# Weights of the RWKV loop brought in by GpSimd DMAs alone: high part cast on the way, low part accumulated from DRAM

## The chip, the cores and the metric

The kernel runs on one core of one Trainium2 chip. The metric is the device time of one execution in microseconds. The kernel before was timed three times: 1142.22, 1146.9 and 1147.43 us, median 1146.9 us.

## What is computed

One layer on 512 tokens of width 1024, all in float32. After an RMS norm one wide product `h @ w_in` gives receptance, keys, values, the two halves of a gated convolution, and two gates. The RWKV-7 time mix runs a recurrence over the tokens for 16 heads of 64 channels (`S = S*w + (S a) b + v k`, `y = S r`); the kernel does it in 8 chunks of 64 tokens. Beside it stands a causal convolution of 31 taps with layer norm and SiLU. Both branches are projected, gated and added; an output projection, a norm with residual, and a SwiGLU feed-forward with 2816 inner channels follow.

Float32 accuracy comes from splitting. A weight `w` is held as a high part `wh`, which is `w` rounded to float32r, and a low part `wl = w - wh`; an activation likewise as `rh + rl`. A product is `wh rh + wh rl + wl rh`: three matmuls of 128 x 128 weights against 128 x 512 activations.

## The kernel before

Channels are tiled by 128, so a product of depth 1024 is 8 such triples. `acc3` (lines 175 to 181) issues one triple: line 179 is `wh rh`, line 180 `wh rl`, line 181 `wl rh`. Weights come in halves: `wload` (lines 162 to 173) fetches 4 tiles side by side, 128 x 512 values or 256 KB, into the buffers `wh` and `wl`, of which there are four each (`WB = 4`). So a half serves 12 matmuls.

`wload` has two forms. Both have SP load the float32 values into a third buffer, `wf` (four of them). In the form used by the loop (`eng is G`), ScalarE (ACT) converts `wf` to `wh` (line 168), ACT writes `-wh` into `wl` (line 169), and a DMA issued by GpSimd (POOL) adds `wf` to it in place (line 170). In the other form ACT converts and VectorE (DVE) subtracts (`split`, lines 158 to 160). The loop's form is used for 106 halves, those whose nominal load position lies between `T0P = 0` and `T1P = 475`; in the trace they are loaded from 47 to 645 us. The start and everything after that use the other form.

The program between is written as a list of small functions with nominal positions (`plan`, `at`), sorted and emitted in that order. Per 128-channel tile there are 44 nominal units: decay, keys, receptance, values (three products of two halves each), masked products inside the chunks (lines 589 to 597), a triangular inverse on DVE (lines 634 and 638), and the chain over the chunks: matmul line 718, ACT copy line 721, matmul line 726, ACT copy line 738, matmul line 744, ACT copy line 751, then the next chunk. Convolution products and taps (line 844) are spread between. A half's load is placed `LEAD = 11` units ahead of its use, or after the last matmul of the half that had its buffers, whichever is later.

Those positions are priorities. Below them a framework orders each engine's instructions by when it expects their inputs, and places all semaphores; each engine then runs its own list strictly in order, and a DMA's wait is done by the engine that issues it.

Of the kernel before, what the change touches and what calls it, by code (L numbers as in the profile page):

```python
# [8 lines left out]
F32 = mybir.dt.float32  # L9
F32R = mybir.dt.float32r  # L10
I32 = mybir.dt.int32
AF = mybir.ActivationFunctionType
ALU = mybir.AluOpType
# [3 lines left out]
P = 128  # L17
# [12 lines left out]
WB = 4  # L30
NWO = 3
BUFS = (2, 2, 2, 2, 1, 1, 1)
# nominal positions that order the program
PERIOD = 44.0
NCL = 3
CPERIOD = 96.0
# [4 lines left out]
WBF = 4  # L41
# [57 lines left out]
def tile_hybrid_block(ctx, tc, xT, cst, prm, dwp, wl1, w2g, w_in, w_ro, w_co, w_o,  # L99
                      w_gt, w_up, w_dn, outT):  # L100
    nc = tc.nc
    V, G, S = nc.vector, nc.gpsimd, nc.scalar
# [9 lines left out]
    wp = ctx.enter_context(tc.tile_pool(name="wp", bufs=WB))  # L112
# [10 lines left out]
    def f(ap):  # L123
        return ap.bitcast(F32)

# [1 line left out]
    cs = cp.tile([P, NC], F32, name="cs")  # L127
    pr = cp.tile([P, NV * NT], F32, name="pr")
    dw = cp.tile([P, NT * KW], F32, name="dw")
# [8 lines left out]
    ones = cs[:, C_ONE:C_ONE + WS]  # L138
# [15 lines left out]

    E, O = slice(0, 64), slice(64, 128)

# [1 line left out]
    def split(src, hi, lo):  # L158
        S.activation(out=hi, in_=src, func=AF.Copy)  # L159
        V.tensor_sub(lo, src, f(hi))  # L160

    def wload(wap, nk, eng=None):
        wf = wp.tile([P, nk * P], F32, tag="wf", bufs=WBF, name="wf")
        wh = wp.tile([P, nk * P], F32R, tag="wh", name="wh")
        wl = wp.tile([P, nk * P], F32R, tag="wl", name="wl")
        nc.sync.dma_start(out=wf, in_=wap)
        if eng is G:
            S.activation(out=wh, in_=wf, func=AF.Copy)  # L168
            S.activation(out=wl, in_=f(wh), func=AF.Copy, scale=-1.0)  # L169
            G.dma_start(out=wl, in_=wf, accum_op=ALU.add)  # L170
        else:
            split(wf, wh, wl)
        return wh, wl

# [27 lines left out]
                     in_=r8.unsqueeze(2).to_broadcast([P, 8, HD]), func=AF.Copy)  # L202
        bcast(ps, lambda b: rx[:, b * P:(b + 1) * P])

    # 1 / sqrt(v) for v > 0: a first guess from the bits, then Newton's steps
    def rsqrt(v, n):
        y, t, w = (sp.tile([P, n], F32, tag=g_, bufs=2, name=g_) for g_ in ("ry", "rt", "rw"))
        V.tensor_scalar(out=y.bitcast(I32), in0=v.bitcast(I32), scalar1=-0.5, scalar2=RSQ,
# [21 lines left out]
        bcast(bc, lambda b: r[:, b:b + 1].to_broadcast([P, P]), blocks)  # L230
        return bc

# [1 line left out]
    ctx_h = ExitStack()  # L234
    hp = ctx_h.enter_context(tc.tile_pool(name="hp", bufs=1))
    HH = hp.tile([P, NT, T + 2], F32R, tag="s1", name="HH")
# [33 lines left out]
    for t_ in (HH, HL):  # L270
        G.memset(f(t_[:, :, 0:2]), 0.0)

    # mean square of x over the channels, per token
    acc = tmp("acc", "ys")

    def sumsq(acc, src, first, name):
# [4 lines left out]
            S.activation(out=sq, in_=src, func=AF.Square)  # L281
            V.tensor_add(acc, acc, sq)

    # the first products take x before its norm, and the norm after them
    ps3 = [p_.tile([P, T], F32, tag=g_, name="dn") for p_, g_ in ((pd, "dn"), (pd, "dn"), (py, "y"))]
    for k in range(NT):
        if k == WK:
# [20 lines left out]
                                   op0=ALU.mult, op1=ALU.mult)  # L308
            split(xs[:, k, :], hh(k), hl(k))

    # derived parameters
    V.tensor_scalar(out=drv[:, 0:3 * NT], in0=vecs("mu_r", 3), scalar1=-1.0, scalar2=1.0,
                    op0=ALU.mult, op1=ALU.add)
    V.tensor_scalar_mul(drv[:, 3 * NT:5 * NT], vecs("decay_w0", 2), 0.5)
# [1 line left out]
    V.tensor_scalar(out=drv[:, 6 * NT:7 * NT], in0=vecs("k_a"), scalar1=-0.5, scalar2=1.0,  # L316
                    op0=ALU.mult, op1=ALU.add)

# [1 line left out]
    ctx_w = ExitStack()  # L320
    Pbd = []
    kp = None
# [11 lines left out]
        nc.sync.dma_start(out=dw, in_=dwp)  # L334
        V.tensor_scalar_mul(dw, dw, 0.5)

    # low-rank inputs: (h + (h_prev - h) mu) W = h (W - mu W) + h_prev (mu W)
    low = {}

    def low_weights(g):  # L340
# [14 lines left out]
    def low_rank(g):  # L355
        t_ = low[g]
        lo_f = tmp("lo_f", "th") if g else ep_.tile([P, T], F32, name="lo_f")
        if g == 0:
            pa, pb_ = (pm.tile([P, T], F32, tag=g_, bufs=1, name="lora") for g_ in ("sb", "fi"))
            for k in range(NT):  # L360
                for q, ps in ((0, pa), (2, pb_)):
                    acc3(ps, t_[:, q, k, :], t_[:, q + 1, k, :], [k], lambda k: XH[:, k, :],
                         lambda k: XL[:, k, :], k == 0, k == NT - 1)
            sh = tmp("sh", "sq", 2)
            V.tensor_mul(lo_f, pa, bx)
            V.tensor_mul(sh, pb_, bx)
            V.tensor_add(lo_f[:, 1:T], lo_f[:, 1:T], sh[:, 0:T - 1])
            S.activation(out=lo_f[E], in_=lo_f[E], func=AF.Tanh)
            # the low parts beside the high ones, under the other half of the rows
            for X, R, Q in ((LH, E, O), (LL, O, E)):  # L370
                S.activation(out=X[R], in_=lo_f[R], func=AF.Copy)
                V.tensor_sub(X[Q], lo_f[R], f(X[R]))
        else:
            ps = pd.tile([P, T], F32, tag="dn", name="lora")
            for k in range(NT):
                for q, rh, rl in ((0, hh, hl), (2, hhs, hls)):
                    acc3(ps, t_[:, q, k, :], t_[:, q + 1, k, :], [k], rh, rl,
                         k + q == 0, k == NT - 1 and q == 2)
            S.activation(out=lo_f, in_=ps, func=AF.Tanh, scale=0.5)
            S.activation(out=lo_f, in_=lo_f, func=AF.Identity, scale=0.5, bias=0.5)  # L380
            split(lo_f, GH, GL)
# [44 lines left out]
    halves = []  # L426
# [21 lines left out]
                fns.append(lambda: then(d["ps"]))  # L448
            halves.append([ts, lambda eng, k0=k0: load(k0, eng), fns])

    # weights are loaded ahead of their use, as far as the buffers go
    def plan_halves():
        halves.sort(key=lambda e: e[0][0])
        for i, (ts, ld, fns) in enumerate(halves):
# [28 lines left out]
    def plan_decay(ct):  # L483
        s_ = st[ct]

        @at(ct, 0.0)
        def _():
            w2h, w2l = low_out(ct, 0, 2 * P, "w2")
            # decay: log w = -exp(-1/2) sigmoid(z)
            zw = pm.tile([P, T], F32, tag="sm", name="zw")  # L490
            low2(zw, w2h[:, 0:P], w2l[:, 0:P], E, LH)
            cum = ktmp("cum")
            S.activation(out=cum, in_=zw, func=AF.Tanh, scale=0.5, bias=der(D_W0H, ct))
            S.activation(out=cum, in_=cum, func=AF.Identity, scale=0.5, bias=0.5)
            V.tensor_tensor_scan(out=cum, data0=reset, data1=cum, initial=0.0,
                                 op0=ALU.mult, op1=ALU.add)
            ep = ktmp("ep", cols=NCH * (L + 1)).rearrange("p (c t) -> p c t", c=NCH)
            G.memset(ep[:, :, 0:1], 1.0)
            S.activation(out=ep[:, :, 1:L + 1], in_=ch3(cum), func=AF.Exp, scale=-C0)
            S.activation(out=cum, in_=cum, func=AF.Exp, scale=C0)  # L500
            dL = sp.tile([P, NCH], F32, tag="dL", bufs=3, name="dL")
            V.tensor_copy(out=dL, in_=ep[:, :, L])
            za = pm.tile([P, T], F32, tag="sm", name="za")
            low2(za, w2h[:, P:2 * P], w2l[:, P:2 * P], O, LL)
            tha = ktmp("tha")
            S.activation(out=tha, in_=za, func=AF.Tanh, scale=0.5, bias=der(D_A0H, ct))
            kf = ktmp("kf")
            S.activation(out=kf, in_=tha, func=AF.Identity, scale=der(D_KAH, ct),
                         bias=der(D_KAO, ct))
            s_.update(cum=cum, ep=ep, dL=dL, tha=tha, kf=kf)  # L510
# [65 lines left out]
    def plan_inner(ct):  # L576
        s_ = st[ct]

        # masked products inside the chunks
        def inner(hc, par):  # L580
            if hc == 0 and par == 0:
                s_["Mt"] = kp.tile([P, NCH, L], F32, tag="Mt", bufs=BUFS[4], name="Mt")
# [17 lines left out]
        for j, (hc, par) in enumerate(((0, 0), (0, 1), (1, 0), (1, 1))):  # L600
            at(ct, 2 * DL + 3.0 + 2.0 * j)(lambda hc=hc, par=par: inner(hc, par))

        # token-major keys
        @at(ct, 2 * DL + 2.0)
        def _():
            bkT = kp.tile([P, NCH, P], F32, tag="bkT", bufs=BUFS[2], name="bkT")
# [7 lines left out]
    def plan_solve(ct):  # L614
        s_ = st[ct]

        # inverse of (I - M) on the 32 x 32 diagonal blocks, one block column class per partition
        @at(ct, 2 * DL + 11.0)
        def _():
            Mt = s_["Mt"]  # L620
# [23 lines left out]
        def _():  # L644
# [3 lines left out]
                        in_=Ps.rearrange("p i q -> p q i"))  # L648
            P32T = kp.tile([P, NCH, B32], F32, tag="P32T", bufs=1, name="P32T")
            V.transpose(out=P32T.rearrange("p c t -> p (c t)"),  # L650
                        in_=P32.rearrange("p c t -> p (c t)"))
            # upper right block: P1 M12 P2
            Wt = kp.tile([P, NCH, B32], F32, tag="Ps", bufs=1, name="Wt")
            R1 = [slice(h * 64, h * 64 + 32) for h in range(2)]
            R2 = [slice(h * 64 + 32, h * 64 + 64) for h in range(2)]
# [20 lines left out]
    def plan_values(ct):  # L676
# [7 lines left out]
        else:  # L684
            plan_dense(ct * PERIOD + 2 * DL, DT, w_in[2 * NT + ct], values)

        # token-major values, centred over the head; bonus
        @at(ct, 3 * DL + 3.0)
        def _():
            tv = s_["bv"]  # L690
# [17 lines left out]
    def plan_chain(ct):  # L708
# [15 lines left out]
        def step1(c):  # L724
            UV, SV, pb, zt, zs = (s_[n] for n in ("UV", "SV", "pb", "zt", "zs"))
            u_ = [PE.matmul(zt[R, 1, :], lhsT=pb[R, c, :], rhs=zs[R], start=True, stop=True)  # L726
                  for R in (E, O)]
            # state before the chunk, under the update
            if 0 < c < NCH - 1:
                s_["old"] = [PE.matmul(zt[R, 2, :], lhsT=ident[R, par * 64:par * 64 + 64],  # L730
                                       rhs=SV[R, c, par, :], start=True,
                                       stop=False, skip_group_check=True)
                             for par, R in ((0, E), (1, O))]
                for a_ in s_["old"]:
                    for b_ in u_:
                        order(a_, b_)
            for par, R in ((0, E), (1, O)):
                S.activation(out=UV[R, c, par, :], in_=zt[R, 1, :], func=AF.Copy)  # L738
# [12 lines left out]
                    S.activation(out=SV[R, c + 1, par, :], in_=zt[R, 2, :], func=AF.Identity,  # L751
                                 scale=dL[R, c:c + 1])

        # output of the chunk
        def step3(c):
            AR, GR, UV, SV, yp = (s_[n] for n in ("AR", "GR", "UV", "SV", "yp"))
            seq = []
# [97 lines left out]
                   plan_chain, plan_finish, plan_conv):  # L855
            pl(ct)

# [1 line left out]
    QT = ("mu_k", "kkn", "tha", "cum", "kf", "ep", "mu_r", "mu_r")  # L859
    HALF = (slice(0, TH), slice(TH, T))  # L860

# [41 lines left out]
        plan_dense(TM + POST + 48 * DTZ * m + 24 * DTZ, DTZ, w_ro[m], lambda ps, m=m: out_r(m, ps),  # L903
                   lambda k: mid["YH"][:, k, :], lambda k: mid["YL"][:, k, :])

    # layer norm over the channels, silu
    TC = max(conv_at(NT - 1) + 2 * CPERIOD2 + 0.1, TM + 2.0)

    def chsum(k):
# [62 lines left out]
    mp = mid["mp"]  # L972
    mh, ml = (lambda k: MH[:, k, :]), (lambda k: ML[:, k, :])

# [1 line left out]
    mo = xp.tile([P, NT, T], F32, tag="x", name="mo")  # L976
    psn = [p_.tile([P, 2, NWO + 1, WS], F32, tag=g_, name="psn") for p_, g_ in ((pc, "ch"), (pm, "sm"))]
    acc = tmp("acc", "ys")
# [59 lines left out]
        residual(m, 0, bc)  # L1038
    bc = all_rstd(psn[1], RMS_EPS, 2)

# [1 line left out]
    psf = [p_.tile([P, T], F32, tag=g_, bufs=1, name="psf")  # L1042
           for p_, g_ in ((pm, "fi"), (pm, "sb"), (pc, "ch"), (py, "y"))]
    for k in range(NT):
# [30 lines left out]
    last = []  # L1075
# [108 lines left out]
```

## Time and profile before

| | |
|---|---|
| timed runs, median | 1146.9 us |
| the profiled execution, first to last instruction (span) | 1165.1 us |
| PE busy, share of the span | 1138.6 us, 98% |
| DVE busy | 721.4 us, 62% |
| ACT busy | 616.5 us, 53% |
| POOL busy | 96.2 us, 8% |
| mean granted TensorE clock | 0.950 of full |
| HBM read | 84.25 MB |

The profiled execution is 18.2 us longer than the median of the timed ones. The span falls into the start (to about 75 us), the loop with the chain (to about 500 us), the end of the loop where the last chain runs beside gate products (to 575 us), a dense stretch of gate and output products that still uses the loop's form of `wload` (to 645 us), and the rest, which the change does not touch. A busy PE is not a PE at its peak: matmuls overlap and their ends are modelled, so how far matmuls start apart says more than the busy time. The TensorE clock has two levels, 1.2 and 2.4 GHz; the granted clock of a stretch is the mean of the two as a share of the upper one.

### The profile page before, as it was taken

The numbers are of one execution on the slowest core, as the hardware profiler recorded it, in microseconds if no ns is written. First come the engines' busy times: TensorE is split into PE (matmuls) and PEld (weight loads), VectorE is DVE, ScalarE is ACT, GpSimd is POOL, SyncE is SP. The second block draws the span as 40 slices with busy tenths as digits, with TensorE's granted clock in tenths as the row PEclk, the third lists the DMA queues.
The fourth block names the chain that finished last, engine by engine and source line by source line (L and its number), as shares of the span: only waits on it lengthen the run. The fifth ranks groups of instructions, "written<-read, shape, count | busy, mean of one in ns | idle before, by whom it ended". The sixth has DMA issues, their size and how long they took to land.

```text
span 1165.1 us, 17942 instructions
## 1 busy us (share of the span) xinstructions
PE 1138.6 (98%) x6506; PEld 869.8 (75%) x6506; DVE 721.4 (62%) x1699; ACT 616.5 (53%) x1291; POOL 96.2 (8%) x140
## 2 busy tenths in 40 slices
PE   7999999999999999999999999999999999999996
PEld 5777675757676767677788788899888888888886
DVE  7968676747776748699698737546444444433324
ACT  6777776758756747564655724535333333333321
POOL 0111010101010101112222000000000000000000
PEclk9999988869988869899999999999999999999998
DMA  7145342524342423356798434500332322333322
GB/s 245 44 100 118 78 98 46 116 46 92 71 100 50 97 69 81 68 125 147 163 203 197 117 99 139 178 19 10 101 98 91 99 91 94 96 91 109 109 64 73
DMA packets 74202, 117.41 MB, mean 101 GB/s; under 512 B 15745, under 2 KB 21249, under 8 KB 74113
## 3 DMA queue, kind: packets, MB, share of 16 engines
q1 hardware_dynamic: 58848, 88.47, 25.2%
q0 software_dynamic: 15264, 27.79, 14.3%
q8 instruction: 51, 0.84, 0.3%
q14 instruction: 39, 0.31, 0.1%
HBM read 84.25 MB, written 2.10 MB: 74 GB/s over the span
## 4 chain that ended last, share of the span: by engine, by line
PE 91%; ACT 4%; DVE 3%; issue 1%; DMA 0%; SPq 0%; DVEq 0%; ACTq 0%
PE dn L179 22%; PE dn L181 22%; PE dn L180 22%; PE gps L589 3%; PE yp L759 2%; PE zt L726 2%; PE zt L718 2%; PE vps L695 1%; PE zt L744 1%; PE yp L763 1%; PE bps L704 1%; PE ss L194 1%; PE psf L180 1%; PE psf L179 1%; PE psf L181 1%
## 5 line engine op out<-in xcount | busy, mean ns | idle before, releaser
L159 ACT ACTIVATE wh<-wf 128x512 fp32r<-128x512 f32 (+1 forms) x172 | 106.6, 621 | 245.5 <-PE dn L180 237.8
L160 DVE TENSOR_TENSOR wl<-wf,wh 128x512 fp32r<-128x512 f32 (+1 forms) x172 | 116.0, 676 | 136.1 <-ACT wh L159 136.1
L179 PE MATMUL dn<-HH,wh 128*128 128x512 f32 x408 | 173.0, 426 | 0.8 <-DVE cpad L823 0.5
L844 DVE SCALAR_TENSOR_TENSOR ca<-cpad,dw,ca 128x512 f32<-128x512 f32 x240 | 171.8, 744 | 1.4
L180 PE MATMUL dn<-HL,wh 128*128 128x512 f32 x408 | 172.1, 422 | 0.0
L181 PE MATMUL dn<-HH,wl 128*128 128x512 f32 x408 | 171.1, 420 | 0.0
L170 POOL DMA_DIRECT2D wl<-wf x106 | 91.6, 870 | 505.3 <-ACT wl L169 325.6
L181 PE MATMUL dn<-FHH,wl 128*128 128x512 f32 x320 | 127.0, 397 | 0.0
L179 PE MATMUL dn<-FHH,wh 128*128 128x512 f32 x320 | 126.6, 395 | 0.0
L180 PE MATMUL dn<-FHL,wh 128*128 128x512 f32 x320 | 125.8, 393 | 0.0
L168 ACT ACTIVATE wh<-wf 128x512 fp32r<-128x512 f32 x106 | 66.3, 629 | 69.1 <-PE dn L180 68.1
L179 PEld LDWEIGHTS dn<-HH,wh 128*128 128x128 f32 x408 | 78.9, 194 | 18.9 <-issue 0.7
L181 PEld LDWEIGHTS dn<-HH,wl 128*128 128x128 f32 x408 | 78.6, 193 | 17.6 <-issue 0.5
L180 PEld LDWEIGHTS dn<-HL,wh 128*128 128x128 f32 x408 | 79.0, 194 | 16.4 <-issue 0.4
L180 PEld LDWEIGHTS dn<-FHL,wh 128*128 128x128 f32 x320 | 60.2, 188 | 15.0
L181 PEld LDWEIGHTS dn<-FHH,wl 128*128 128x128 f32 x320 | 60.1, 188 | 14.5
L179 PEld LDWEIGHTS dn<-FHH,wh 128*128 128x128 f32 x320 | 60.0, 188 | 13.8
L169 ACT ACTIVATE wl<-wh 128x512 fp32r<-128x512 f32 x106 | 66.3, 628 | 2.1 <-ACT UV L738 0.4
L179 PE MATMUL dn<-FH,wh 128*128 128x512 f32 (+1 forms) x166 | 64.3, 387 | 0.0
L181 PE MATMUL dn<-FH,wl 128*128 128x512 f32 (+1 forms) x166 | 64.1, 386 | 0.0
L180 PE MATMUL dn<-FH,wh 128*128 128x512 f32 (+1 forms) x166 | 64.1, 386 | 0.0
L638 DVE TENSOR_TENSOR Ps<-Ps,tt 128x60 f32<-128x60 f32 (+24 forms) x248 | 52.6, 212 | 3.4
(303 smaller groups left out, 2111.0 us busy)
## 6 DMA issues: line engine op xcount, KB each, us to landing
wf<-in_w_in_dram SPq DMA_DIRECT2D x112, 256.0 KB, 3.1
wl<-wf POOLq DMA_DIRECT2D x106, 256.0 KB, 3.7
wf<-in_w_gt_dram SPq DMA_DIRECT2D x44, 256.0 KB, 2.6
wf<-in_w_up_dram SPq DMA_DIRECT2D x44, 256.0 KB, 2.8
wf<-in_w_dn_dram SPq DMA_DIRECT2D x40, 256.0 KB, 2.7
wf<-in_w_ro_dram SPq DMA_DIRECT2D x16, 256.0 KB, 3.0
wf<-in_w_co_dram SPq DMA_DIRECT2D x16, 256.0 KB, 2.6
wf<-in_w_o_dram SPq DMA_DIRECT2D x16, 256.0 KB, 2.9
```

What stands on the lines that cost most here:

```text
L159: S.activation(out=hi, in_=src, func=AF.Copy)
L160: V.tensor_sub(lo, src, f(hi))
L168: S.activation(out=wh, in_=wf, func=AF.Copy)
L169: S.activation(out=wl, in_=f(wh), func=AF.Copy, scale=-1.0)
L170: G.dma_start(out=wl, in_=wf, accum_op=ALU.add)
L179: PE.matmul(ps, lhsT=a, rhs=rh(k), start=first and j == 0, stop=False)
L180: PE.matmul(ps, lhsT=a, rhs=rl(k), start=False, stop=False)
L181: PE.matmul(ps, lhsT=b, rhs=rh(k), start=False, stop=last and j == n - 1)
L589: PE.matmul(ps[:, c, :], lhsT=bk[R, hc * 4 + c, :], rhs=AR[R, hc * 4 + c, par:par + 2, :], start=True, stop=True)
L638: solved[0] = V.tensor_add(Ps[:, 0:j, q0:8], Ps[:, 0:j, q0:8], tt)
L718: PE.matmul(zt[R, 0, :], lhsT=AR[:, c, 2 * par, :], rhs=SV[:, c, par, :], start=True, stop=True)
L844: a_ = V.scalar_tensor_tensor(out=o_, in0=cb[:, j:j + T], scalar=tap(j), in1=o_, op0=ALU.mult, op1=ALU.add)
```

## The change

In the loop's form of `wload` the load into `wf` by SP and the conversion by ACT go. A DMA issued by POOL writes `wh` directly from DRAM, casting float32 to float32r. ACT's `-wh` stays. The accumulating DMA of POOL now takes its source from DRAM and not from `wf`. The other form is as it was. Comments elsewhere are removed, which changes nothing.

```diff
     def wload(wap, nk, eng=None):
-        wf = wp.tile([P, nk * P], F32, tag="wf", bufs=WBF, name="wf")
         wh = wp.tile([P, nk * P], F32R, tag="wh", name="wh")
         wl = wp.tile([P, nk * P], F32R, tag="wl", name="wl")
-        nc.sync.dma_start(out=wf, in_=wap)
         if eng is G:
-            S.activation(out=wh, in_=wf, func=AF.Copy)
+            G.dma_start(out=wh, in_=wap)
             S.activation(out=wl, in_=f(wh), func=AF.Copy, scale=-1.0)
-            G.dma_start(out=wl, in_=wf, accum_op=ALU.add)
+            G.dma_start(out=wl, in_=wap, accum_op=ALU.add)
         else:
+            wf = wp.tile([P, nk * P], F32, tag="wf", bufs=WBF, name="wf")
+            nc.sync.dma_start(out=wf, in_=wap)
             split(wf, wh, wl)
         return wh, wl
```

## Rows read from the trace of the kernel before

**Rows 1.** The stages: busy time of each engine, granted clock, DMA share, GB/s
```profile
75.00:500.00 425.00, 419.26 (x2973) 286.99 (x2973) 293.29 (x961) 287.45 (x705) 53.38 (x77) 0.87 0.37 81
500.00:575.00 75.00, 74.79 (x483) 52.88 (x482) 62.83 (x108) 42.42 (x97) 17.24 (x20) 1.00 0.66 142
575.00:645.00 70.00, 70.00 (x315) 56.98 (x314) 62.59 (x107) 41.77 (x73) 19.83 (x23) 1.00 0.90 199
```
**Rows 2.** ACT's costliest groups in the loop, 75 to 500 us
```profile
L169 ACT ACTIVATE wl<-wh 128x512 fp32r<-128x512 f32 x59 | 37.0, 628 | 1.4 <-ACT UV L738 0.4 <-ACT g2h L159 0.2
L168 ACT ACTIVATE wh<-wf 128x512 fp32r<-128x512 f32 x59 | 36.9, 629 | 26.3 <-PE dn L180 25.6
```
**Rows 3.** PE's waits for ACT in the loop: total us, times, longest
```profile
PEld yp L759 <- ACT SV L751: 9.4, 25, 0.7
...
PEld zt L726 <- ACT cum L493: 1.1, 2, 0.7
```
**Rows 4.** Two stretches of the loop, columns as in Rows 1
```profile
225.00:275.00 50.00, 50.00 (x289) 31.99 (x288) 28.30 (x105) 30.37 (x75) 5.33 (x9) 0.73 0.26 54
275.00:325.00 50.00, 49.59 (x408) 34.35 (x407) 38.76 (x126) 39.43 (x98) 5.66 (x10) 1.00 0.39 85
```
**Rows 5.** Line 170, whole span, then 575 to 645 us: issue to landing
```profile
DMA to landing us min/median/max: 3.2/3.7/6.2
...
DMA to landing us min/median/max: 3.3/4.1/6.0
```
**Rows 6.** Line 166, SP's loads from 45 to 645 us: issue to landing
```profile
DMA to landing us min/median/max: 2.4/3.0/4.9
```
**Rows 7.** ACT in order of time, the loop at 205 us: start, duration
```profile
206.83 1.17 ACT L168 ACTIVATE wh<-wf 128x512 fp32r<-128x512 f32 x2
207.88 1.16 ACT L169 ACTIVATE wl<-wh 128x512 fp32r<-128x512 f32 x2
```
**Rows 8.** POOL in order of time, the loop
```profile
207.26 0.86 POOL L170 DMA_DIRECT2D wl<-wf  x1 [8.12 <-ACT wl L169]
...
217.27 0.86 POOL L170 DMA_DIRECT2D wl<-wf  x1 [2.38 <-ACT wl L169]
```
**Rows 9.** PE's weight loads: first use of the low parts issued at 207.26 and 217.27
```profile
212.42 0.19 PEld L181 LDWEIGHTS dn<-HH,wl 128*128 128x128 f32 x1
...
254.20 0.19 PEld L181 LDWEIGHTS dn<-HH,wl 128*128 128x128 f32 x1
```
**Rows 10.** Issue to landing of the two DMAs of Rows 8
```profile
DMA to landing us min/median/max: 3.4/3.4/3.4
...
DMA to landing us min/median/max: 4.4/4.4/4.4
```
**Rows 11.** One half in the dense stretch: PE's release, ACT, POOL, first uses
```profile
604.79 0.39 PE L180 MATMUL dn<-YL,wh 128*128 128x512 f32 x1
...
605.21 0.63 ACT L168 ACTIVATE wh<-wf 128x512 fp32r<-128x512 f32 x1 [1.48 <-PE dn L180]
605.88 0.63 ACT L169 ACTIVATE wl<-wh 128x512 fp32r<-128x512 f32 x1
608.00 0.63 ACT L168 ACTIVATE wh<-wf 128x512 fp32r<-128x512 f32 x1 [1.49 <-PE dn L180]
...
606.80 0.86 POOL L170 DMA_DIRECT2D wl<-wf  x1 [1.91 <-ACT wl L169]
...
613.36 0.19 PEld L179 LDWEIGHTS dn<-YH,wh 128*128 128x128 f32 x1
613.83 0.19 PEld L181 LDWEIGHTS dn<-YH,wl 128*128 128x128 f32 x1
```
**Rows 12.** DMA queues of the whole span: packets, MB, share of 16 engines
```profile
q1 hardware_dynamic: 58848, 88.47, 25.2%
q0 software_dynamic: 15264, 27.79, 14.3%
```

## The prediction, as put on record

> **What bounds the kernel now.** I read the stage table first. In the loop PE is busy 419 of 425 us, but DVE and ACT are busy two thirds of it as well and the clock is at 0.87 [rows 1]: PE there waits on a serial chain and drops to its lower clock in between, so the loop is bounded by short waits, not by matmuls alone. In the dense stretch from 575 us PE is at full clock without a gap, and the DMA engines are 0.90 busy [rows 1]. There PE sets the time: one half begins every 2.79 us (605.21 to 608.00 in the ACT rows [rows 11]). The change touches three things: ACT's load, the time from a free weight buffer to a landed low part, and what the DMA engines do. After 645 us it touches nothing.
>
> So the question is how long before its use a half's low part lands now. I pair each issue at line 170 with the first line 181 weight load that waits on its semaphore. In the loop the tightest issue is at 207.26, lands 3.4 us later, at 210.67, and is used at 212.42: 1.75 us of cover. A loose one is issued at 217.27, lands 4.4 later and is used at 254.20 [rows 8 to 10]. Of 60 pairs in the loop six have under 3.1 us (1.75, 1.99, 2.10, 2.42, 2.96, 3.08), the median has 12. Of 19 pairs between 500 and 575 us four have less than 3.1 (1.09, 1.52, 1.64, 2.48), of 26 in the dense stretch eleven.
>
> **ACT: what goes.** 106 conversions go, 59 of them in the loop, 36.9 of ACT's 287.45 us there [rows 1, 2], 13%. ACT is not the bound. It matters where a chain copy queues behind a conversion. PE stands 40 us in the loop for ACT, the sum of twelve entries of which the first and the last are shown [rows 3]; if queueing shrinks with the load, 13% of 40 is 5 us gained. Bounds: 0, if no waiting copy stands behind a conversion, and 36.9, if every conversion does. I take 5, since the entries are mostly short waits of 0.4 to 0.7 us that a copy and its signal take anyway. ACT's own wait for the buffer (25.6 us before line 168 [rows 2]) moves to POOL.
>
> **The new wait.** Now `wh` is converted 0.67 us before `-wh` can start (605.21 to 605.88 [rows 11]), because `wf` is loaded long before. Afterwards POOL can issue the cast only when the buffer is free, and the load from DRAM lies uncovered in the path. The trace has no casting DMA. Its landing is bounded by SP's plain load, 2.4 us at the least, 3.0 at the median [rows 6], and by POOL's accumulation of equal size, 3.7 at the median and 6.2 at the most [rows 5]. I take 3.7: same issuer, same queue, same bytes. With 0.1 for the semaphore, each low part comes 3.7 + 0.1 - 0.67 = 3.1 us later (1.8 to 5.6).
>
> Loop: the six tight pairs fall short of 3.1 by 1.35, 1.11, 1.00, 0.68, 0.14 and 0.02, in sum 4.3 us. 500 to 575 us: 2.01 + 1.58 + 1.46 + 0.62 = 5.7 us. The other pairs have cover.
>
> Dense stretch: every half is alike, and a delay comes back only when the same buffer comes round, every fourth half. The high part's last reader starts at 604.79 and takes 0.39; the low part is wanted at 613.83 [rows 11], 8.65 us after. The path: 0.1, cast 4.1 (the median of this stretch [rows 5]), 0.05, ACT 0.63, 0.29 until POOL issues (605.88 + 0.63 to 606.80), accumulation 4.1: 9.27 us, late by 0.62. 26 halves are 6.5 rounds, 4.0 us. With both landings at 3.3 it would be nothing, with both at 6.0 some 4.4 a round, 29 us.
>
> Sum 4.3 + 5.7 + 4.0 = 14.0 us. Bounds: 1.4 at the fastest load (only the pairs of 1.09, 1.52, 1.64 and 1.75 fall short, by 0.1 to 0.8), and at 6.2 some 32 + 34 + 29 = 95. PE could hide up to six matmuls' worth by taking lines 179 and 180 of all four tiles first, 1.4 us a half; I count nothing for it, as the order follows expected, not measured landings.
>
> **Who is behind the new waits.** ACT's `-wh` now waits for a DMA, and chain copies queue behind it. Instructions are not in program order: at 206.83 two conversions run and then two negations [rows 7], so I expect the negation to be put where the cast should have landed, and charge only the lateness above. POOL issues two DMAs a half, 106 more of 0.86 us. It is busy 53 of 425 us in the loop and 19.8 of 70 in the dense stretch [rows 1]; doubled it still has room, and its few memsets get later by at most one issue. Cost 0, if POOL's list puts the cast of the next half ahead of the accumulation of this one (rival 3 if not). SP loses 106 loads, and no engine waits there: 0.
>
> **DMA engines.** A packet of the software queue costs 0.143 x 16 x 1165.1 / 15264 = 0.175 us, of the hardware queue 0.252 x 16 x 1165.1 / 58848 = 0.080 [rows 12]. An accumulation (144 packets, 9 an engine) takes each engine 1.57 us, a load 0.72, 2.29 of a dense half's 2.79. The cast reads one stream, like the load, and I count it as one: 0. As dear as an accumulation it would make 3.14 a half, 0.35 over, 26 x 0.35 = 9 us; that is the other bound. HBM is read twice for each half, 27 MB more; in the dense stretch 199 GB/s are moved as it is [rows 1], of which a part from buffer to buffer now comes from DRAM; I count nothing beyond that bound.
>
> **Sum.** 14.0 - 5 = +9 us: 1165.1 becomes 1174 in the profiled execution. That one is 18.2 us over the median of the timed runs; the sum is a difference and goes onto the median: 1146.9 + 9 = 1156.
>
> **Rivals.** (1) The cast is hidden. It lands as the plain load's median, 3.0: each low part is 2.4 us later, the loop falls short by 1.1, the next stretch by 1.31 + 0.88 + 0.76 = 3.0, the dense one has 0.1 + 3.0 + 0.05 + 0.63 + 0.29 + 4.1 = 8.17 against 8.65 and loses nothing. 4 - 5 = -1: 1146. For it: same bytes from the same DRAM. Against: another issuer, and a queue shared with accumulations.
> The Trainium skill, page "DMA: Bandwidth & Descriptors", section "Anatomy of one DMA — SWDGE (gpsimd) path", gives a software DMA about 2.0 us plus its bytes at 436 GB/s, an estimate of 2.6 us for 256 KB; by that the low parts would come 2.0 us later, some 2 us would be lost and the sum would be -3, 1144. The trace does not agree for accumulations: none of 106 lands under 3.2 [rows 5].
>
> (2) Faster, on the other side. The ACT queue, relieved of its conversions and of the buffer wait, lets the chain run closer, and PE's matmuls then stand dense enough that the clock falls less often. Place: the loop. At 0.73 PE did 289 matmuls in 50 us, at 1.00 it did 408 [rows 4]; 27 us at the lower clock cost 119 / 408 x 50 = 14.6 us, 0.54 each. The loop has (1 - 0.87) x 2 x 425 = 110 us at the lower clock; a quarter less gives 15, with the 5 above 20: 1127. It decides as soon as ACT's relief in the chain exceeds the 14 us of late weights. For it: a copy behind a conversion loses up to 0.63. Against: the relief on the rows is 5, and a late weight opens gaps that lower the clock just as well.
>
> (3) Much slower: POOL's list has the cast of a half behind the accumulation of the half before. Then each half costs the whole round on POOL: 3.7 + 0.05 + 0.63 + 0.29 + 0.86 = 5.5 us against 2.79, 2.7 x 45 halves from 500 us on: +122, near 1270; in a third of them 1190. For it: POOL runs its list in order. Against: the order follows expected times.
>
> That the change would not do what it says (a copy in place of a cast) would alter the values, not these times.
>
> **Chances.** Forecast 0.42, its own range 1148 to 1170; rival 1 0.20; rival 2 0.25; rival 3 with a dear cast 0.13. About 0.5%, 5.7 us, is what a measurement of this kernel can tell from no change: 1141.2 to 1152.6. Faster: rival 2 and the lower end of rival 1, 0.30. Same: the rest of rival 1 and the lower end of the forecast, 0.25. Slower: 0.45. The range, 1128 to 1188, leaves out half of rival 2 and most of rival 3.
>
> **What would show it.** Right: in the dense stretch halves begin more than 2.79 us apart, PE's line 181 waits for the accumulating DMA, landings of the cast near 3.7, 106 fewer ACT instructions and PE's waits for ACT in the loop near 35 us. Wrong: no wait of PE for a DMA anywhere, or ACT standing for `wh` so long that the chain's copies are late; a granted clock in the loop over 0.9 (rival 2); POOL idle before line 170's casts with free buffers (rival 3).

## Result and profile after

The changed kernel takes 1227.4 us (median of three: 1215.6, 1227.4, 1242.6), before 1146.9: 1.064 times as long, 95% interval 1.054 to 1.074. Slower was forecast, but by 9 us and with an upper bound of 1188; it is 80 us.

The page of the profiled execution, with ACT's and POOL's groups of a half (busy and mean ns, then idle time ahead of them and what ended most of it). Lines move by two: 166 is the cast, 167 the negation, 168 the accumulation.
```profile
span 1225.6 us, 17733 instructions
PE 1172.2 (96%) x6506; PEld 886.3 (72%) x6506; DVE 721.3 (59%) x1699; ACT 557.9 (46%) x1185; POOL 156.0 (13%) x246
PEclk9997887997596969799999989999999999999999
PE 69%; issue 12%; DMA 6%; POOL 5%; ACT 4%; DVE 4%; POOLq 0%; SPq 0%; DVEq 0%; ACTq 0%
L167 ACT ACTIVATE wl<-wh 128x512 fp32r<-128x512 f32 x106 | 66.5, 630 | 123.5 <-DMA wh<-in_w_in_dram 93.3
L168 POOL DMA_DIRECT2D wl<-in_w_in_dram x96 | 84.6, 899 | 202.4 <-ACT wl L167 162.3
L166 POOL DMA_DIRECT2D wh<-in_w_in_dram x96 | 58.0, 610 | 302.8 <-PE dn L180 145.2
wh<-in_w_in_dram POOLq DMA_DIRECT2D x96, 256.0 KB, 3.5
wl<-in_w_in_dram POOLq DMA_DIRECT2D x96, 256.0 KB, 4.1
```
ACT loses its 106 conversions (616.5 to 557.9 us busy) and PE gains nothing from it. ACT now stands 123.5 us ahead of the negation, most of it for the cast. Ahead of a half's first ACT instruction, the conversion, it stood 69.1 us over the span before, nearly all of it for PE to free the buffer:
```profile
L168 ACT ACTIVATE wh<-wf 128x512 fp32r<-128x512 f32 x106 | 66.3, 629 | 69.1 <-PE dn L180 68.1
```
DMA and POOL have entered the chain that ends last. The landings are about as forecast: 3.5 for the cast (3.7 was taken), 4.1 for the accumulation.

The stages of the same execution, columns as in [rows 1], cut where the work of the old stages ends:
```profile
75.00:525.00 450.00, 433.28 (x2929) 294.79 (x2927) 285.85 (x932) 252.76 (x642) 84.20 (x133) 0.83 0.38 75
525.00:618.00 93.00, 85.71 (x513) 59.60 (x511) 67.96 (x132) 32.98 (x80) 30.33 (x43) 0.96 0.61 120
618.00:700.00 82.00, 75.47 (x322) 56.34 (x318) 61.74 (x104) 27.85 (x49) 32.63 (x46) 1.00 0.80 169
```
The waits, whole span (us in total, times, longest):
```profile
POOL wl L168 <- ACT wl L167: 183.0, 73, 5.7
ACT wl L167 <- DMA wh<-in_w_in_dram: 93.3, 49, 5.1
ACT wl L167 <- DMA wh<-in_w_ro_dram: 19.4, 7, 4.3
PEld dn L181 <- DMA wl<-in_w_in_dram: 14.4, 17, 2.3
PEld dn L181 <- DMA wl<-in_w_ro_dram: 7.3, 7, 2.3
```
POOL waits for ACT, ACT for the cast, and the cast is a DMA of POOL.

**Where the 60 us between the two profiled executions lie.** As marks I take the first squares (line 785) of the seventh and of the eighth channel tile, the issue of the last weight DMA of POOL, and the end:

| us | 7th tile | to the 8th | to the last DMA | to the end |
|---|---|---|---|---|
| before | 494.1 | 80.5 | 66.9 | 523.6 |
| after | 524.9 | 93.3 | 82.6 | 524.8 |
| difference | +30.8 | +12.8 | +15.7 | +1.2 |

Half is lost in the loop, half behind it, and the two halves are lost in different ways.

**The dense stretch, step by step.** POOL's list from 676 to 690 us (start, duration, line, and in brackets the wait ahead of it), then ACT's negations of the same time:
```profile
676.18 0.87 POOL L168 DMA_DIRECT2D wl<-in_w_in_dram  x1 [1.66 <-ACT wl L167]
676.75 0.86 POOL L166 DMA_DIRECT2D wh<-in_w_ro_dram  x1
679.56 0.87 POOL L168 DMA_DIRECT2D wl<-in_w_in_dram  x1 [1.95 <-ACT wl L167]
680.11 0.87 POOL L166 DMA_DIRECT2D wh<-in_w_ro_dram  x1
682.33 0.87 POOL L168 DMA_DIRECT2D wl<-in_w_ro_dram  x1 [1.35 <-ACT wl L167]
683.32 0.54 POOL L166 DMA_DIRECT2D wh<-in_w_in_dram  x1
686.99 0.87 POOL L168 DMA_DIRECT2D wl<-in_w_ro_dram  x1 [3.12 <-ACT wl L167]
```
```profile
678.63 0.63 ACT L167 ACTIVATE wl<-wh 128x512 fp32r<-128x512 f32 x1 [2.26 <-DMA wh<-in_w_in_dram]
681.40 0.64 ACT L167 ACTIVATE wl<-wh 128x512 fp32r<-128x512 f32 x1 [2.14 <-DMA wh<-in_w_ro_dram]
686.06 0.63 ACT L167 ACTIVATE wl<-wh 128x512 fp32r<-128x512 f32 x1 [4.02 <-DMA wh<-in_w_ro_dram]
```
The list alternates. Behind the accumulation of one half stands, with no gap, the cast of the half two further on: issued at 676.75, its negation runs at 681.40, its accumulation at 682.33, and right behind that the next cast of the same row. So a round goes issue, landing, negation, accumulation: 6.15 us (676.18 to 682.33) or 7.43 (679.56 to 686.99) for two halves. PE needs 5.58 for two [rows 11]. Over 26 successive halves PE's first line 181 weight load goes from 612.56 to 703.36, 3.49 us a half. The same halves before go from 568.76 to 645.75, 2.96 a half (2.79 where nothing else lies between two halves): 0.53 too much, 14 us in 26.

Landings of cast and accumulation from 618 to 700 us (minimum, median, maximum):
```profile
DMA to landing us min/median/max: 3.4/4.6/5.9
DMA to landing us min/median/max: 3.7/4.3/5.7
```

**The loop.** Its marks differ also between executions without any cast, so I set beside each the time that PE spent at the lower of its two clock levels before the seventh tile's mark (from the trace's clock records):

| kernel | 7th tile, us | at the lower level, us | mark less half of that |
|---|---|---|---|
| before | 494.1 | 109 | 439.5 |
| e1 (only the DRAM source) | 473.8 | 65 | 441.4 |
| e12 (unread cast) | 474.1 | 61 | 443.4 |
| e6 (cast ahead) | 484.9 | 82 | 444.0 |
| e13 (form of before, other buffer counts) | 500.4 | 109 | 445.7 |
| e3 (changed in the loop only) | 513.2 | 123 | 451.7 |
| e7 (negation on POOL) | 522.6 | 157 | 444.1 |
| after | 524.9 | 154 | 448.1 |
| e5 (five buffers) | 530.1 | 167 | 446.4 |
| e2 (only the cast) | 535.3 | 174 | 448.3 |

Less half of the time at the lower level, ten marks that lie up to 61 us apart come within 12 of each other. Of the other six runs four fall near the same band (e9 438.6, e11 440.6, e4 442.9, e14 446.4); e8 (456.6) and e10 (461.0) do not. Of the loop's +30.8 us, (154 - 109) / 2 = 22 are clock and 8.6 are longer waits. In the loop PE stands for no accumulating DMA. Its waits for ACT and those of its weight loads sum to 71.8 us there, 58.7 before. The profiled execution of before had itself more of the lower level than e1's, whose PE, ACT and DVE run the same instructions in the same order, but for one pair of neighbouring matmuls: some 20 us from one execution to the next.

### The profile page after: what moved, and what is told of

The parts are those of the page before. It is cut to its first block, busy times and chain, and to the rows that moved or that the text cites. A ratio compares the mean times of both kernels' runs of the same rounds, so it can differ in the third digit from the quotient of the medians.

```text
span 1225.6 us, 17733 instructions
## 1 busy us (share of the span) xinstructions
PE 1172.2 (96%) x6506; PEld 886.3 (72%) x6506; DVE 721.3 (59%) x1699; ACT 557.9 (46%) x1185; POOL 156.0 (13%) x246
## 4 chain that ended last, share of the span: by engine, by line
PE 69%; issue 12%; DMA 6%; POOL 5%; ACT 4%; DVE 4%; POOLq 0%; SPq 0%; DVEq 0%; ACTq 0%
PE dn L179 16%; PE dn L181 16%; PE dn L180 16%; DMA wh<-in_w_in_dram 4%; POOL wl L168 3%; PE gps L589 2%; PE yp L759 2%; POOL wh L166 2%; PE zt L726 1%; PE vps L695 1%; PE zt L718 1%; PE bps L704 1%; PE zt L744 1%; PE ss L194 1%; PE yp L763 1%
## 5 line engine op out<-in xcount | busy, mean ns | idle before, releaser
L181 PE MATMUL dn<-HH,wl 128*128 128x512 f32 x408 | 174.7, 429 | 7.7 <-DMA wl<-in_w_in_dram 7.4
L179 PE MATMUL dn<-HH,wh 128*128 128x512 f32 x408 | 175.9, 432 | 2.1 <-DVE mu_k L399 1.7
L167 ACT ACTIVATE wl<-wh 128x512 fp32r<-128x512 f32 x106 | 66.5, 630 | 123.5 <-DMA wh<-in_w_in_dram 93.3
L168 POOL DMA_DIRECT2D wl<-in_w_in_dram x96 | 84.6, 899 | 202.4 <-ACT wl L167 162.3
L181 PEld LDWEIGHTS dn<-HH,wl 128*128 128x128 f32 x408 | 79.6, 195 | 31.3 <-DMA wl<-in_w_in_dram 14.4
L166 POOL DMA_DIRECT2D wh<-in_w_in_dram x96 | 58.0, 610 | 302.8 <-PE dn L180 145.2
L179 PEld LDWEIGHTS dn<-HH,wh 128*128 128x128 f32 x408 | 79.9, 196 | 20.4 <-DVE mu_k L399 2.1
```

Of the source, the lines that this page charges most:

```text
L166: G.dma_start(out=wh, in_=wap)
L168: G.dma_start(out=wl, in_=wap, accum_op=ALU.add)
L179: PE.matmul(ps, lhsT=a, rhs=rh(k), start=first and j == 0, stop=False)
L181: PE.matmul(ps, lhsT=b, rhs=rh(k), start=False, stop=last and j == n - 1)
```

## Experiments

In every ratio a number under 1 is quicker than the kernel before; intervals are 95%.

### e1, e11: only the accumulation's source
```diff
-            G.dma_start(out=wl, in_=wf, accum_op=ALU.add)
+            G.dma_start(out=wl, in_=wap, accum_op=ALU.add)
```


> The high part as before (SP loads the float32 buffer, ACT converts it); only the accumulation takes its source from DRAM. Theory A (the cast stands uncovered between the free buffer and the negation, and holds ACT's and POOL's queues): 1140 to 1155 us, no wait of PE for a DMA. Theory B (reading DRAM in the accumulation is dear: it lands at 4.1 us in place of 3.7, and HBM is read twice): above 1190. Theory C (any edit of these lines reorders the loop and moves the clock, whatever the DMAs do): a granted clock under 0.94 and 1160 to 1200.

1144.5 us, 0.9945 (0.990 to 0.999). The source is not the cost. The run was repeated to see if the gain is real:

> The kernel of before with the accumulation reading DRAM instead of the float32 buffer, once more. Its first time was 0.9945 of before's, with an interval that ends at 0.999. A real gain of that size: 0.990 to 0.998 again. No gain: 0.998 to 1.004.

1151.3 us, 1.0014 (0.9965 to 1.0063). It is not; this half of the change does nothing that can be measured.

### e2: only the cast
SP still loads `wf`, and the accumulation reads it.
```diff
-            S.activation(out=wh, in_=wf, func=AF.Copy)
+            G.dma_start(out=wh, in_=wap)
```


> The high part cast by POOL from DRAM as in the changed kernel; SP still loads the float32 buffer, and the accumulation takes it from there. Theory A: 1200 to 1240 us, like the changed kernel, with ACT standing over 100 us for the cast. Theory B: 1140 to 1160. Theory C: 1160 to 1240, with a clock under 0.94.

1244.8 us, 1.081 (1.073 to 1.090): the whole loss, and a little more; that the load that stayed costs the rest is not shown. ACT's wait for the cast:
```profile
ACT wl L169 <- DMA wh<-in_w_in_dram: 108.6, 51, 6.0
```

### e3, e4: the change in one stretch
`TZ - LEAD` (nominal 361) parts the loop's halves from those of the gate and output products; halves on the other side keep the form of before.
```diff
-            at(0, t_)(lambda ld=ld, i=i, t_=t_: ld(G if T0P < t_ < T1P else None))
+            at(0, t_)(lambda ld=ld, i=i, t_=t_: ld(("old" if t_ < TZ - LEAD else G) if T0P < t_ < T1P else None))
```
(e4; e3 with `>=`.)

> The changed form only for halves placed before nominal position 361 (the loop with the chain, to about 500 us); the later ones in the form of before. Theory A: the loop has the larger part of the loss, by ACT's wait for the cast in front of the chain's copies and by the lower clock: 1175 to 1200 us, and the dense stretch back at 2.79 us a half. Theory C: all of the loss, near 1220.

> The form of before to nominal position 361, the changed form only for the later halves. Theory A: the last chain and the dense stretch lose 25 to 35 us by PE's wait for the accumulation, at full clock: 1170 to 1185 us, near 3.5 us a half. Theory C: nothing, 1140 to 1155.

e3 1199.6 us, 1.035 (1.023 to 1.047); e4 1176.3, 1.020 (1.010 to 1.030). Together 5.5% of 6.4: both stretches lose. In e4 the loop ends at 471.9 us, and the two stages behind it take 97.1 and 85.4 us; in e3 they take 79.9 and 66.9, as before.

### e6: the cast planned ahead
Six high buffers; the cast stands 5 nominal units ahead of the negation, or where its buffer comes free. To make room there are three float32 buffers instead of four. The part that places the cast (the rest sets the numbers of buffers and gives the cast a function of its own):
```diff
+            if T0P < t_ < T1P:
+                t_c = ts[0] - LEAD - PRE
+                if i >= WBH:
+                    t_c = max([t_c] + [e[0][WK - 1] + 0.001 for e in halves[:i - WBH + 1]])
+                at(0, min(t_c, t_))(lambda ld=ld: ld("cast"))
             at(0, t_)(lambda ld=ld, i=i, t_=t_: ld(G if T0P < t_ < T1P else None))
```


> The changed kernel with the load's lead given back: six high buffers in place of four, the cast placed 5 units ahead of the negation, and three float32 buffers in place of four to make room (they are used outside the loop only). Two high buffers more let a cast run about two halves ahead. Theory A1 (the cast is uncovered between the free buffer and the negation): ACT's wait for the cast falls from 122 us below 40, time 1140 to 1175. Theory A2 (POOL's list, in which casts and accumulations wait for one another, is what costs): stays above 1200. Theory C (the new order and the clock): stays above 1190.

1173.0 us, 1.021 (1.012 to 1.029): two thirds of the loss are gone. Its stages behind the loop, its waits from 565 to 632 us, and there the landings of cast and accumulation:
```profile
485.00:565.00 80.00, 79.73 (x510) 57.23 (x511) 67.44 (x131) 33.19 (x81) 30.28 (x43) 1.00 0.69 139
565.00:632.00 67.00, 67.00 (x302) 54.72 (x303) 60.36 (x103) 28.11 (x49) 31.29 (x44) 1.00 0.91 198
```
```profile
ACT wl L174 <- PE dn L188: 34.9, 19, 2.8
POOL wh L166 <- PE dn L188: 24.2, 21, 2.4
POOL wl L175 <- ACT wl L174: 12.6, 23, 4.1
...
ACT wl L174 <- DMA wh<-in_w_in_dram: 2.3, 1, 2.3
```
```profile
DMA to landing us min/median/max: 3.2/4.3/5.8
...
DMA to landing us min/median/max: 3.7/4.8/6.1
```
The same DMAs in the same number, landing no sooner in sum than after the change (4.3 and 4.8 against 4.6 and 4.3), and these stages are as short as before (80.0 and 66.3 us to the marks). ACT now waits for PE to free a buffer, not for a DMA. So the 28 us lost there go when the cast stands further ahead and has two more buffers to land in; what it moves is not the cost. The next run takes a deeper buffer alone.

### e5: deeper buffers, the cast where it was
```diff
-WB = 4
+WB = 5
-WBF = 4
+WBF = 3
```


> The changed kernel with five buffers a half instead of four, high and low (and three float32 buffers instead of four for what still uses them). The cast still stands one place ahead of its negation in the program. Theory A in its first form (the cast lies uncovered between its planned place and the negation, whatever the depth): in the dense stretch casts may go one half earlier, so 1180 to 1225. If a free buffer were all that is missing, 1150 to 1175; if the depth does nothing, 1215 to 1245.

1235.9 us, 1.075 (1.068 to 1.083). A fifth buffer alone gains nothing: 93.1 us from the seventh tile's mark to the eighth's, as after the change, and a loop with 167 us at the lower clock level. From the eighth mark on, POOL issues a cast in the median 2.8 us after PE's last read of the buffer, 0.7 us after the change: what the fifth buffer gives is lost in POOL's list. Six high buffers with the cast where it was were not run.

### e9: the buffers of e5 without the cast
e1 with `WB = 5` and `WBF = 3`.

> The version with the high part from the float32 buffer and the accumulation from DRAM, which lets go of a float32 buffer as soon as ACT has converted it: three of those in place of four, and five weight buffers in place of four. Theory A: as cover is what counts, more of it does no harm and gains little, as PE already waits for no DMA there: 1130 to 1150. If the order matters more than cover (theory C): 1150 to 1190.

1148.9 us, 0.999 (0.994 to 1.004): neither the depth nor the missing float32 buffer does anything where the accumulation reads DRAM.

### e7, e8: another engine for the negation
```diff
-            S.activation(out=wl, in_=f(wh), func=AF.Copy, scale=-1.0)
+            G.tensor_scalar_mul(wl, f(wh), -1.0)
```
(e7; e8 with `V`, which is DVE.)

> The changed kernel with the negation on POOL in place of ACT: nothing of ACT waits for the cast any more, while the way from a free buffer to a landed low part gets no shorter (POOL takes about 1 us or more for the negation). If ACT's queue, stopped by the cast, is what delays the loop: the loop gets back 30 us or more of its 50, the dense stretch stays at 3.5 us a half or worse: 1185 to 1205. If late weights alone delay the loop: 1225 or more.

> The changed kernel with the negation on DVE in place of ACT. DVE then stands for the cast; its inverse and taps are less in the chain's way than ACT's copies. If ACT's stopped queue is the loop's cause: 1190 to 1215. If late weights alone are: 1215 to 1235 as the changed kernel.

e7 1269.3 us, 1.107 (1.101 to 1.113): its loop ends as after the change (522.6), though ACT no longer waits for a cast, and the two stages behind it take 121.5 and 108 us. There POOL itself stands for each cast, with the next cast behind it, and its negation takes 1.49 us where ACT's took 0.63. e8 1206.2, 1.049 (1.041 to 1.058). By the recorded expectations e7 speaks for late weights and e8 for ACT's stopped queue, so the two together do not decide. What they show is smaller: PE's waits for ACT in the loop fall from 71.8 us to 57.5 (e7) and 46.2 (e8), so the negation's wait for the cast does put some 13 us of waits on PE; and e7's loop is as long without them, by 157 us at the lower clock level. e8's gain of some 20 us is all in the granted clock (0.924 to 0.958 against 0.916 to 0.940 after the change): span times granted clock is 1140.5 us in the median of its executions, 1138.6 after the change.

### e10, e12: a cast that nobody reads
e1's form with a cast of each half into a scratch buffer besides, and three float32 buffers instead of four. In e10 the cast stands ahead of the conversion. In e12, shown here, GpSimd first copies eight columns of the converted half there, which holds the cast at its half.
```diff
             S.activation(out=wh, in_=wf, func=AF.Copy)
+            wx = wp.tile([P, nk * P], F32R, tag="wx", bufs=2, name="wx")
+            G.tensor_copy(out=wx[:, 0:8], in_=f(wh)[:, 0:8])
+            G.dma_start(out=wx, in_=wap)
```


> The kernel of before with the accumulation reading DRAM, and besides a cast of every half from DRAM into a buffer that nothing reads, at the cast's place in GpSimd's list (the float32 load, ScalarE's conversion and negation stay). It has the cast's traffic and its share of GpSimd's list, and nobody waits for it. Theory A (what costs is that the negation waits for the cast's landing): the time of the version with only the DRAM source, 1144.5, up to 1160 for the queue behind the cast. Rival D (the traffic and the longer queue of GpSimd are the cost, by whomever they are awaited): 1185 to 1240. The order of the instructions may shift with the added issue, which would blur it by some 10 us.

1184.2 us, 1.031 (1.024 to 1.038), but it doesn't test what it was meant to: with nothing to hold them, 87 of the 106 casts were issued before 190 us (71 of them after 40 us), and accumulations stood behind them. Most of the loss is in the first tile (the mark of the first tile is at 183.7 us against 144.2).

> The unread cast again, now held at its half: ahead of it GpSimd copies eight columns of the converted half into the scratch buffer, so the cast of a half can only be issued once ScalarE has converted that half, just ahead of its accumulation (in the run before, the program ran 71 of the 96 unread casts ahead, before 190 us). GpSimd's list has copy, cast, accumulation for each half; nobody but the next but one cast waits for a cast. Theory A (the wait of the negation for the cast costs): 1145 to 1165, and the dense stretch from 575 us as long as before (66 to 70 us). Rival D (the cast's traffic and the longer queue, whoever waits): 1185 to 1240 and a dense stretch of 75 to 85 us.

1177.9 us, 1.026 (1.016 to 1.036). Its two halves answer differently. The loop ends at 474.1, as e1's: the cast's traffic and its place in POOL's queue cost the loop nothing as long as nobody waits for it. Behind the loop it takes 97.5 and 79.6 us:
```profile
474.10:571.70 97.60, 85.08 (x511) 59.58 (x511) 68.11 (x132) 44.48 (x102) 57.28 (x64) 0.93 0.74 167
571.70:651.00 79.30, 72.42 (x306) 56.53 (x306) 60.73 (x103) 41.00 (x71) 51.80 (x69) 0.96 0.99 250
```
Here three transfers a half (load, cast, accumulation) fill the DMA engines (0.99), and the accumulations land 6.9 us after their issue. The changed kernel has two, at 0.80. So this loss is likely another one, and does not bear on the changed kernel's.

### e13, e14: the cast ahead in one stretch
e6's form on one side of `TZ - LEAD`, the form of before on the other (e13: ahead behind the loop; e14: ahead in the loop).

> The form of before for the loop's halves (float32 load, conversion, accumulation from the float32 buffer), the changed form with the cast planned 5 units ahead only in the dense stretch after; six high buffers, three float32 ones. The same split without the cast ahead was 1.0201 of before. Theory A (in the dense stretch only the cast's place costs): 0.997 to 1.005 of before. If the cast's share of GpSimd's list and of the queue costs whatever its place: 1.01 to 1.02.

> The other split: the changed form with the cast planned 5 units ahead for the loop's halves only, the form of before in the dense stretch after. Without the cast ahead this split was 1.0351 of before, and cast ahead in both stretches 1.0206. Theory A (the cast's place is the loop's loss too): 0.997 to 1.010. Rival C (what is left of the loop's loss is the new order of the instructions and the clock that it gets, which the cast's place doesn't mend): 1.015 to 1.025, all of what is left when the cast is ahead in both stretches.

e13 1182.3 us, 1.033 (1.022 to 1.045); e14 1200.8, 1.057 (1.045 to 1.068). Both sums miss, and the stages show why. e13 has the cast ahead behind the loop, and there it loses nothing (79.9 and 66.3 us), as expected of the place. It loses in the loop, which has the form of before: 500.4, with 109 us at the lower clock level. Only the numbers of buffers differ there, and with them the order of the instructions; ACT also stands 11.7 us for float32 loads. e14's loop is e6's (487.4); it loses behind it (83.5 and 79.5), where the form of before now has three float32 buffers:
```profile
ACT wh L175 <- DMA wf<-in_w_in_dram: 45.4, 21, 4.8
```
In that form the accumulation holds the float32 buffer until it has landed, so three are too few where halves follow each other closely; where it reads DRAM they were enough (e9). The splits therefore don't test what they were meant to.

## Why the prediction was wrong

**"Who is behind the new waits"** is the step that failed. Two costs stood there at nothing, and a third, the clock, stood outside the sum.

"I expect the negation to be put where the cast should have landed": ACT stood 122 us for the cast (93.3, 19.4 and 9.7 put down to issue). And POOL's was 0, "if POOL's list puts the cast of the next half ahead of the accumulation of this one". It puts it behind, not of the half just before, as rival 3 had it, but of the half two before. That is rival 3 at half strength: 6.15 to 7.43 us for two halves where it had 5.5 for one. I had its price (the round on POOL) and treated it as a condition to be met instead of reading from the program that cast and negation are planned at one and the same place, so that nothing puts a landing between them. In e6, with the cast planned further ahead and two more high buffers, both stages are as short as before; in e5, with one more buffer and the cast where it was, neither is.

**Dense stretch.** The term of 0.62 us a round of four halves became 0.53 a half, and 15.7 us between the marks in place of 4.0. From PE's last read of a high buffer to the use of the low part four halves later the working had 9.27 us; the trace has 11.5 in the mean of the 23 halves from 618 to 700 us. The cast was taken to be issued 0.1 us after the buffer comes free: POOL issues it 1.04 after, in 10 of the 23 after 0.30, in most of the others behind an accumulation that waits for an earlier cast. The two landings, 4.1 each in the working, take 4.60 and 4.47, so they are mis-sized by about as much. From the seventh tile to the eighth it is 12.8 instead of 5.7; some 3 of it are 6.8 us at the lower clock level.

**Loop.** The six tight pairs were to give 4.3 us, but PE waits for no accumulating DMA there; the 8.6 us of longer waits came mostly by ACT (71.8 us of PE's waits against 58.7), whose cost stood at nothing. The larger part, 22 us, is the clock, which stood only in rival 2, and there as a gain. Its counter-argument, that "a late weight opens gaps that lower the clock just as well", had the direction right; that the lateness does it is not shown. An example from the loop of the changed kernel, ACT first and then POOL, DVE and PE:
```profile
99.22 0.64 ACT L167 ACTIVATE wl<-wh 128x512 fp32r<-128x512 f32 x1
104.67 0.63 ACT L167 ACTIVATE wl<-wh 128x512 fp32r<-128x512 f32 x1 [4.82 <-issue]
105.21 1.67 ACT L666 ACTIVATE Pbd<-P 32x256 f32<-32x256 f32 x4
```
```profile
99.22 0.88 POOL L166 DMA_DIRECT2D wh<-in_w_in_dram  x1
```
```profile
103.53 0.71 DVE L647 STREAM_TRANSPOSE P<-Ps 128x256 f32<-128x256 f32 x1
```
```profile
108.43 0.69 PE L670 MATMUL xps<-P,Wt 32*32 32x32 f32 x32 [1.12 <-ACT Wt L662]
```
The cast issued at 99.22 lands at 104.60; the negation stands 4.82 us for it, and the copies of the inverse (line 666) stand behind the negation. Their input is there at 104.24 (DVE's transpose, line 647) and they start at 105.21, 0.97 us later; PE stands 1.12 us for the copies behind them (line 662). From 110.2 us the clock is at its lower level for 24 us. The stretch around it, 100 to 115 and 115 to 140 us, in the changed kernel, in e1, in e13, in e6 and before:
```profile
100.00:115.00 15.00, 13.15 (x116) 9.64 (x115) 10.40 (x28) 8.38 (x21) 3.84 (x6) 0.84 0.59 116
115.00:140.00 25.00, 25.00 (x132) 15.69 (x130) 11.51 (x38) 12.30 (x34) 1.43 (x2) 0.62 0.23 42
```
```profile
100.00:115.00 15.00, 14.30 (x152) 10.97 (x151) 11.89 (x32) 11.81 (x31) 2.60 (x3) 1.00 0.50 102
115.00:140.00 25.00, 25.00 (x200) 15.29 (x198) 18.50 (x62) 18.58 (x52) 2.89 (x5) 1.00 0.40 83
```
```profile
100.00:115.00 15.00, 13.18 (x136) 9.89 (x135) 11.82 (x33) 10.87 (x27) 2.06 (x3) 1.00 0.35 79
115.00:140.00 25.00, 25.00 (x111) 15.79 (x113) 11.08 (x36) 12.58 (x32) 2.09 (x3) 0.52 0.32 64
```
```profile
100.00:115.00 15.00, 13.74 (x120) 10.39 (x119) 10.74 (x27) 9.75 (x24) 4.26 (x6) 0.83 0.45 95
115.00:140.00 25.00, 25.00 (x139) 15.12 (x137) 12.84 (x46) 12.00 (x33) 1.41 (x2) 0.63 0.25 48
```
```profile
100.00:115.00 15.00, 14.30 (x140) 10.95 (x141) 11.91 (x34) 11.88 (x29) 2.59 (x3) 0.93 0.41 86
115.00:140.00 25.00, 25.00 (x187) 15.91 (x186) 15.54 (x54) 17.24 (x48) 2.59 (x3) 0.90 0.34 69
```
In the changed kernel and in e13 PE has about one microsecond less of work than in e1, and in the 25 us that follow 132 or 111 matmuls run where e1 runs 200. But e13 has the form of before in its loop, and e6's ACT waits for no cast there, and both fall in the same place; before falls a little with as much work as e1. So the clock falls there without a wait for a cast as well, and these rows do not show that the wait is the cause. That gaps lower the clock goes by their order in time alone; no run changed the gaps alone.

**What held.** The direction, in part by luck: most of the loss came by terms that stood at nothing. The landings over the whole span. PE's waits for the accumulating DMA and halves more than 2.79 us apart in the dense stretch. The DMA engines at no cost: 0.80 busy against 0.90 in [rows 1]. HBM read twice at no cost (e1). **What else did not:** the 5 us from ACT's relief. In the loop PE's and its weight loads' waits for ACT sum to 72 us, 59 before (all entries of that view from 75 us to the seventh tile's mark; the prediction's 40 are the twelve longest of the weight loads). They are 56 in e6, where the cast is ahead, and 58 and 46 in e7 and e8, where the negation is not on ACT: the relief went, and more, into copies that stand behind the negation. Rivals 1 and 2 fell with the first trace. (Rival 1's 1.1 us for the loop is 1.4 by its own pairs, which changes nothing.)

**The size against the medians** is 80 us, 20 more than between the profiles, because the profiled execution of before had much of the lower clock level. The experiments' records give span and granted clock of every execution, and their product is the span less half of the time at the lower level. In 53 executions of before, of 1137 to 1171 us, it is 1104 to 1112, 8 us apart where the spans are 35; in the three of the changed kernel 1137 to 1141; in the four of e6 1107 to 1113. So of the 80 us some 30 are longer waits and some 50 the clock. The longer waits are the ones that the POOL round and the copies behind the negation account for, and in e6 hardly any of them is left.

**What stays open.** e6 is still 26 us over before in its median, though its profiled execution (1159.3 us) has no wait of PE for a DMA and a loop 9 us shorter than the profiled one of before. By the products above what remains is the clock (0.925 to 0.960 against 0.968 in the median of before). That the loop's new order brings it is suggested by e13, whose loop has no cast, and not shown; the kernel emits its order from nominal positions, and no run here held the order and moved the cast alone. Of the loop's 31 us I can say which part is clock, not how much of that the uncovered casts brought and how much the new order. No version beats the kernel before.

## What to carry to other kernels

When a DMA takes over what an engine did, its latency moves into the path of whoever comes next; look where in the issuing engine's list the DMA stands, and plan it a landing ahead of its reader, with buffers for that. A list that alternates "wait for the reader of the last DMA" and "issue the next" can be no faster than the round: here 6.15 to 7.43 us for two halves that PE works through in 5.58. Where the granted clock is not at its upper level throughout, forecast it as a term of its own, and compare spans times granted clock beside the spans: here the clock had 50 of the 80 us, and a profile of one execution can mislead by 20.

## What was not expected of the hardware

The lower clock level differs between executions of the same instructions on PE, ACT and DVE: 65 and 75 us of it in the loop in two of the version with only another DMA source, and 109 in one of before, by spans of 1145.3, 1149.2 and 1165.1 us. The 53 executions of before have a granted clock of 0.944 to 0.980. The Trainium skill ("TensorE: Matmul & The Clock Gate", "What's actually happening") says of the matmuls at a kernel's start that how many run at the lower clock varies from run to run; the traces show such a difference in the middle of a kernel. The Trainium skill, in the same section, puts that loss at the start at under 1% of a typical kernel's span. The loop's falls are not covered by that figure: its 109 us cost 55, 4.7% of the span.

A cast of 256 KB landed 2.7 us after its issue at the least, 3.6 in the median of all, and 4.6 where casts and accumulations follow each other on POOL's queue. The issue of a cast stands in POOL's rows with 0.54 us alone (683.32) and with 0.86 right behind an accumulation (676.75), whose own row it overlaps by 0.30.
